# Six PSUM banks as one tile in an attention and SwiGLU layer, with priority for what empties a bank and later input builds

## The chip, the cores and the metric

The kernel runs on one core of one Trainium2 chip. The metric is the device time of one execution, in microseconds (us). A core has a matrix engine (TensorE, PE in the profile, with its weight loads as PEld), a vector engine (VectorE, DVE), a scalar engine (ScalarE, ACT), a general engine (GpSimd, POOL) and a queue engine (SyncE, SP) from which this kernel issues nearly all its transfers. TensorE writes its results to PSUM, which has eight banks of 128 partitions x 512 fp32 values; VectorE and ScalarE read them there.

## The reference

One layer of a streaming encoder on x, 2048 tokens of width 1024, in float32. The layer adds two normalised branches to x:

```python
h = rms_norm(x, g_pre_mix);  m = chunk_relpos_attention(h, w_qkv, w_o, rel_bias)
x = x + rms_norm(m, g_post_mix)
h = rms_norm(x, g_pre_ffn)
x = x + rms_norm((silu(h @ w_gate) * (h @ w_up)) @ w_down, g_post_ffn)     # 1024 -> 2816 -> 1024
```

The attention has 16 heads of width 64. Tokens stand in chunks of 64, and a query reads its own chunk and the eight before it, with a learned bias by clipped distance:

```python
for c in range(n_chunks):                       # 32 chunks of 64 queries
    k0, k1 = max(0, (c - 8) * 64), (c + 1) * 64
    sc = q[c] @ k[k0:k1].T / 8 + bias
    out[c] = softmax(sc) @ v[k0:k1]
```

## The kernel before, in words

**Tiles and stages.** The tokens are cut into four quarters of 512. Dense products run as three products of split numbers (a high and a low part for each operand, lines 197 to 199), and the large ones (values, queries and keys, gate and up, down) use a scheme of seven block products on 2 x 2 blocks, named B11, B21, T1, T2, B22, T3 and T4; the class `Blocks` builds their inputs with ACT and DVE. In time the kernel runs: projections for two groups of two quarters (`project`, 0 to 498.7 us), attention (498.7 to 1107), the output projection of the last quarter (`o_quarter`, from 1107), and the feed-forward part up to the end.

**Attention.** Quarters run in the order 1, 0, 2, 3. In each, eight jobs of one pair of heads run, and each job has four slots of 128 queries. A slot `t` of the loop issues:

- `transposed(t)`: four 128 x 128 transposes of the first head's probabilities, then four of the second's (L548). DVE copies the first to SBUF (L551), ACT the second (L553).
- `scaled(t + 2)`: DVE takes a reciprocal of the row sums (L530), POOL scales two heads' probabilities (L533).
- `scores(t + 3)`: eight matmuls (L508 and L509) write two heads' scores, 640 keys each. DVE adds the bias and reduces, one instruction per head (L517); ACT takes the exponential, one per head (L521).
- `fifth(t)`: the fifth key block's two transposes (L562), copied by ACT (L563). Quarter 0 has no earlier quarter, so its slots have fewer key blocks and no fifth.
- every fourth slot, `output()`: PV of the job before, 32 matmuls (L578) into `po`; ACT copies it as the high part (L584), and DVE subtracts that for the low part (L585).

Between these, `fill` puts in dense matmuls of the output projection of the quarter before, three at a time. The first quarter that runs has no such work.

**PSUM in attention.** Pool `psa` holds `st` (three banks, one buffer, the scores of both heads), `tt` (one bank, two buffers) and `po` (one bank). Two more banks belong to pool `ps` (tag "mm", two buffers), which the dense work uses.

**What sets the order.** PE runs in the order of the code (a manual schedule). The other engines' instructions are ordered by the tile framework's scheduler, by priority, which follows the order of the code unless a block of code raises it. Semaphores between the engines are put in by the framework, from the tiles that an instruction reads and writes. Work on other engines that prepares a later stage stands in a list `later`; `tick` takes it off as PE's work is issued, at a cost that each step names. Weights come by `fetch` (two 512 KB loads on SP's queue) and are split by `part_split` (L131 on ACT, L132 on DVE).

Of the kernel before, what the change touches and what calls it, by code (L numbers as in the profile page):

```python
# [17 lines left out]
P = 128  # L18
# [31 lines left out]
def trunk(  # L50
# [18 lines left out]
    class sp:  # L69
        @staticmethod  # L70
        def dma_start(dst, src):
            last_sp[0] = nc.sync.dma_start(dst, src)

# [370 lines left out]

    class Attend:


        def __init__(self, n, p):
            self.n, self.p = n, p
            self.prev = n > 0  # L450
            self.sc = {}
            self.pT = None

# [37 lines left out]
        def scores(self, ib):  # L491
# [19 lines left out]
            for h in range(2):  # L511
# [5 lines left out]
                dve.tensor_tensor_reduce(  # L517
# [19 lines left out]
        def transposed(self, ib):  # L537
# [6 lines left out]
            for h in range(2):  # L544
                part = blocks[:4]
                tt = phase["psa"].tile([P, 4, P], F32, tag="tt", name="tt", bufs=2)
# [3 lines left out]
                if h == 0:  # L550
                    dve.tensor_copy(dst, tt[:, : len(part), :])  # L551
                else:
                    act.activation(dst, tt[:, : len(part), :], AF.Copy)  # L553
            self.rest = (sc, blocks[4], cols) if self.prev else None

        def fifth(self):
# [6 lines left out]
            act.activation(self.pT[:, :, 4, cols], tt[:, 0:2, :], AF.Copy)  # L563

        def output(self):
# [8 lines left out]
            po = phase["psa"].tile([P, HALF], F32, tag="po", name="po", bufs=1)  # L574
# [9 lines left out]
            act.activation(ats[n].hi(p), po, AF.Copy)  # L584
            return lambda: dve.tensor_tensor(ats[n].lo(p), po, ats[n].hi(p).bitcast(F32), op=ALU.subtract)  # L585

    def o_quarter(n):
# [4 lines left out]
        for d2 in range(KT // 2):  # L592
# [3 lines left out]
            for dt in (2 * d2, 2 * d2 + 1):  # L596
# [10 lines left out]
                act.activation(t, pt, AF.Copy)  # L607
# [3 lines left out]
    class Blocks:  # L611
# [53 lines left out]
        def put(self, name, k, src):  # L665
            if name not in self.t:
                self.t[name] = hb_tile(self.slot[name])
            split(self.t[name][:, 0, k, :], self.t[name][:, 1, k, :], src)

        def build(self, part, w, prep):  # L670
# [17 lines left out]

            def b11(k):
                prep(0, k, at("T3", 1, k))  # L690
                self.put("B11", k, at("T3", 1, k))

            def b21(k):
                prep(0, k + 4, at("T4", 1, k))
                self.put("B21", k, at("T4", 1, k))

            def t1(k):
# [3 lines left out]
                self.put("T1", k, a)  # L701

            def t2(k):
# [3 lines left out]
                dve.tensor_tensor(a, c, a, op=ALU.add)  # L707
                self.put("T2", k, a)
                dve.tensor_tensor(b, b, c, op=ALU.subtract)
                dve.tensor_tensor(a, d, a, op=ALU.subtract)  # L710
# [205 lines left out]
    def gate_up(g, b):  # L916
# [22 lines left out]
        for c in range(NC):  # L939
# [6 lines left out]
            def copy(pts, dst):  # L946
                return lambda i: act.activation(dst[i], pts[i], AF.Copy)
# [4 lines left out]
            def c11(i):  # L952
                if i == 0:
                    t["B11"] = narrow("b11")
                    act.activation(t["B11"], pa[0], AF.Silu)
                else:
                    finish(t["B11"], pa[1])
                    put("B11")

            def u(i):  # L960
                dve.tensor_tensor(u2[i], p1[i], pb[i], op=ALU.subtract)
                dve.tensor_tensor(p5[i], p5[i], p1[i], op=ALU.add)

            def closing(pts, terms, then, op=ALU.subtract):
                def go(i):
                    dve.tensor_tensor(terms[i], pts[i], terms[i], op=op)  # L966
# [47 lines left out]
    def down(g, store, between=lambda n: None):  # L1014
# [42 lines left out]
        def copy(pts, to):  # L1057
            return lambda d, _: act.activation(to[d], pts[d], AF.Copy)

        def add(a, b_, op=ALU.add):  # L1060
            return lambda dst: dve.tensor_tensor(dst, a, b_, op=op)
# [17 lines left out]
        def u(d, _):  # L1079
            if not end:  # L1080
                u2[d] = narrow("u2")
            dve.tensor_tensor(u2[d], p1[d], pc[d], op=ALU.subtract)
# [10 lines left out]
        def c22(d, _):  # L1093
            dve.tensor_tensor(u3[d], pc[d], p1[d], op=ALU.subtract)
# [83 lines left out]
    def values_of(g, b, big):  # L1178
# [4 lines left out]
        def put(n, m, u, a, b_, op=ALU.add):  # L1183
            t = narrow("v")
            dve.tensor_tensor(t, a, b_, op=op)
            emit_v(n, m, u, t)

        def after(name, m, pt):
            if name == "B11":
                act.activation(p1[m], pt, AF.Copy)  # L1190
            elif name == "B21":
                put(s0, m, 0, pt, p1[m])
            elif name == "T1":
                act.activation(z[m], pt, AF.Copy)
# [482 lines left out]
```

## Time and profile before

| | |
|---|---|
| runs (us) | 2447.67, 2444.43, 2446.71; median 2446.71 |
| profiled execution (us) | 2446.41 |
| its span in the profile (us) | 2444.6 |
| mean granted clock of TensorE | 0.991 |
| PE busy | 2347.2 us, 96% of the span, 11480 matmuls |
| DVE, ACT, POOL busy | 1644.1, 1163.2 and 316.7 us |
| DMA | 529.72 MB, mean 217 GB/s |

A row of the windows view gives a stretch's length, then for PE, PEld, DVE, ACT and POOL the busy time and (x) the instructions, then the clock that TensorE was granted as a share of full speed, the share of the DMA engines that was busy, and GB/s. A row of the timeline gives start, length, engine, line and operation, output <- inputs, shape; in brackets stands the idle time before it and the instruction that ended it. A group's row gives line, engine, operation and count, then busy time and the mean of one in ns, then the idle time before. Ends of matmuls are modelled, and consecutive matmuls overlap, so the step from one start to the next is read for their cost in a row.

### The profile page before, as it was taken

The numbers are of one execution on the slowest core, as the hardware profiler recorded it, in microseconds if no ns is written. First come the engines' busy times: TensorE is split into PE (matmuls) and PEld (weight loads), VectorE is DVE, ScalarE is ACT, GpSimd is POOL, SyncE is SP. The second block draws the span as 40 slices with busy tenths as digits, with TensorE's granted clock in tenths as the row PEclk, the third lists the DMA queues.
The fourth block names the chain that finished last, engine by engine and source line by source line (L and its number), as shares of the span: only waits on it lengthen the run. The fifth ranks groups of instructions, "written<-read, shape, count | busy, mean of one in ns | idle before, by whom it ended". The sixth has DMA issues, their size and how long they took to land.

```text
span 2444.6 us, 33016 instructions
## 1 busy us (share of the span) xinstructions
PE 2347.2 (96%) x11480; PEld 1903.1 (78%) x11480; DVE 1644.1 (67%) x2625; ACT 1163.2 (48%) x2039; POOL 316.7 (13%) x422
## 2 busy tenths in 40 slices
PE   8999899989999899998999999999999999999998
PEld 6887688866676676767887888888888888888887
DVE  7775856666665556667876777677657667555567
ACT  8443733357665555664433333365433333334454
POOL 1012110023334324330000000000000000000002
PEclk9999999999999999999999999999999999999999
DMA  7699997678798878946666544287666757446654
GB/s 281 215 293 311 306 274 233 186 208 226 198 230 234 261 207 227 246 139 235 230 210 238 194 173 167 101 268 240 213 219 202 235 158 239 137 169 233 193 187 153
DMA packets 229782, 529.72 MB, mean 217 GB/s; under 512 B 26320, under 2 KB 42720, under 8 KB 225136
## 3 DMA queue, kind: packets, MB, share of 16 engines
q1 hardware_dynamic: 217712, 480.42, 62.6%
q0 software_dynamic: 11904, 47.19, 6.5%
q8 instruction: 91, 1.49, 0.3%
q14 instruction: 75, 0.61, 0.1%
HBM read 380.14 MB, written 170.44 MB: 225 GB/s over the span
## 4 chain that ended last, share of the span: by engine, by line
PE 54%; DVE 2%; issue 2%; DMA 1%; ACT 1%; POOL 0%; SPq 0%; DVEq 0%; ACTq 0%; POOLq 0%
PE pd L199 6%; PE pd L198 6%; PE pd L197 6%; PE pb L197 4%; PE pb L199 4%; PE pb L198 4%; PE pc L199 3%; PE pc L198 3%; PE pc L197 3%; PE pa L198 3%; PE pa L199 3%; PE pa L197 3%; PE po L578 1%; PE mm L199 1%; PE mm L197 1%
## 5 line engine op out<-in xcount | busy, mean ns | idle before, releaser
L533 POOL TENSOR_SCALAR sc<-sc,rows 128x640 f32<-128x640 f32 (+4 forms) x256 | 195.6, 777 | 364.7 <-DVE rows L530 221.9
L521 ACT ACTIVATE sc<-sc,rows 128x640 f32<-128x640 f32 (+4 forms) x256 | 192.9, 755 | 88.6 <-DVE rows L517 88.1
L517 DVE CUSTOM_DVE_ANT_0 sc<-st,bias 128x640 f32<-128x640 f32 (+2 forms) x248 | 173.6, 734 | 57.0 <-PE st L509 31.9
L197 PE MATMUL pb<-hb,w_wg_T 128*128 128x512 f32 x528 | 206.4, 391 | 3.8 <-DVE terms L966 3.8
L199 PE MATMUL pb<-hb,w_wg_T 128*128 128x512 f32 x528 | 206.2, 391 | 0.0
L198 PE MATMUL pb<-hb,w_wg_T 128*128 128x512 f32 x528 | 206.1, 390 | 0.0
L548 PE MATMUL tt<-ident,sc 128*128 128x128 f32 x928 | 135.0, 278 | 34.3 <-DVE pT L551 10.2
L548 PEld LDWEIGHTS tt<-ident,sc 128*128 128x128 f32 x928 | 105.1, 141 | 76.9 <-issue 45.0
L508 PE MATMUL st<-k,q 128*128 128x384 f32 (+3 forms) x432 | 137.4, 338 | 14.4 <-DVE rows L517 13.1
L199 PE MATMUL pd<-a,w_d_T 128*128 128x512 f32 (+1 forms) x368 | 139.9, 380 | 0.1
L197 PE MATMUL pd<-a,w_d_T 128*128 128x512 f32 (+1 forms) x368 | 139.9, 380 | 0.0
L198 PE MATMUL pd<-a,w_d_T 128*128 128x512 f32 (+1 forms) x368 | 139.8, 380 | 0.0
L551 DVE COPY pT<-tt 128x512 f32<-128x512 f32 (+3 forms) x128 | 81.5, 637 | 83.7 <-PE tt L548 63.6
L198 PE MATMUL pa<-hb,w_wg_B 128*128 128x512 f32 x352 | 136.9, 389 | 0.0
L197 PE MATMUL pa<-hb,w_wg_B 128*128 128x512 f32 x352 | 136.9, 389 | 0.0
L199 PE MATMUL pa<-hb,w_wg_B 128*128 128x512 f32 x352 | 136.9, 389 | 0.0
L968 ACT ACTIVATE terms<-terms 128x512 f32<-128x512 f32 x65 | 41.1, 632 | 182.5 <-DVE terms L966 182.5
L131 ACT ACTIVATE w_wg_T<-raw 128x1024 fp32r<-128x1024 f32 x88 | 92.9, 1057 | 71.9 <-PE pa L199 35.1
L509 PE MATMUL st<-k,q 128*128 128x384 f32 (+3 forms) x432 | 126.9, 314 | 0.0
L354 DVE TENSOR_TENSOR a<-raw_a,a 128x512 fp32r<-128x512 f32 x154 | 105.5, 692 | 25.2 <-ACT a L353 24.8
L289 POOL TENSOR_TENSOR rs<-ms,neg_half 128x4 f32<-128x4 f32 (+1 forms) x7 | 8.4, 1201 | 863.9 <-DVE ms L287 863.9
L197 PEld LDWEIGHTS pb<-hb,w_wg_T 128*128 128x128 f32 x528 | 99.5, 188 | 25.8 <-issue 4.6
(265 smaller groups left out, 6248.9 us busy)
## 6 DMA issues: line engine op xcount, KB each, us to landing
raw<-in_w_gu SPq DMA_DIRECT2D x77, 512.0 KB, 4.2
q<-q SPq DMA_DIRECT2D x62, 512.0 KB, 6.7
k<-k SPq DMA_DIRECT2D x54, 512.0 KB, 9.0
s_g_S<-raw POOLq DMA_DIRECT2D x44, 512.0 KB, 3.0
raw_d<-d_S SPq DMA_DIRECT2D x88, 256.0 KB, 3.6
raw_a<-aT SPq DMA_DIRECT2D x88, 256.0 KB, 3.5
raw<-s_g_S SPq DMA_DIRECT2D x44, 512.0 KB, 4.2
bias<-ext_d SPq DMA_DIRECT2D x124, 144.0 KB, 9.0
```

Source lines behind the costliest of these rows:

```text
L131: act.activation(hi, raw, AF.Copy)
L197: pe.matmul(pt, a_hi, b_hi, start=first, stop=False, skip_group_check=go_on)
L198: pe.matmul(pt, a_hi, b_lo, start=False, stop=False, skip_group_check=go_on)
L199: pe.matmul(pt, a_lo, b_hi, start=False, stop=last, skip_group_check=go_on)
L354: eng.tensor_tensor(lo, src, hi.bitcast(F32), op=ALU.subtract)
L508: pe.matmul(st[:, a:b], q[:, 2 * h, cols], kk[:, h, key], start=True, stop=False)
L509: pe.matmul(st[:, a:b], q[:, 2 * h + 1, cols], kk[:, h, key], start=False, stop=True)
L517: dve.tensor_tensor_reduce(out=sc[:, :n], in0=st[:, c0 : c0 + n], in1=rev, scale=-1.0, scalar=3.0e38, op0=ALU.add, op1=ALU.min, accum_out= ...
L521: act.activation(sc[:, :n], sc[:, :n], AF.Exp, bias=nmax, scale=-1.0, accum_out=rows[:, h : h + 1])
L533: last_pool[0] = pool.tensor_scalar(sc[:, :n], sc[:, :n], rows[:, 2 + h : 3 + h], 1.0, op0=ALU.mult, op1=ALU.mult)
L548: pe.transpose(tt[:, u, :], sc[h][:, b * P : b * P + P], ident)
L551: dve.tensor_copy(dst, tt[:, : len(part), :])
```

## The change

Five things change.

1. `Soon` wraps ACT and DVE so that an instruction issued through it has the scheduler's priority of 150 instructions earlier. It is used for what reads a PSUM bank: the reductions of scores, the copies of transposes and PV, and the first readers of the block products. In the changed kernel such instructions have the helper's line, L85.
2. One tile of six banks, `banks`, takes the place of `st`, `tt` and `po`. In the quarters after the first, the scores take banks 0 to 2, and the first head's transposes, the second's, the fifth block's and PV take banks 3, 4 and 5 in turn. In the first quarter the transposes of four go to the "mm" buffers of pool `ps`, the fifth block's to bank 4 and PV to bank 5, and each head's scores are cut as 512 + 128, in banks 0 and 1 for the first head and 2 and 3 for the second. Before, and in the later quarters, they are cut as 384 + 256 and 256 + 384, and the two heads share the middle bank.
3. In `project` the 32 ACT instructions that scaled x by the gain are gone; the gain is a factor of the instructions that build the blocks (an ACT copy with a scale, and a DVE scalar-tensor-tensor). The warm-up matmuls go from 28 to 20, and the steps for the row roots of group 0 and 1 wait longer between by-token sums and their transposes (2 to 14, and 2 to 8 units).
4. The second group's blocks are built later: B21 behind product B22 of the first group's queries and keys (it was T2), and T1, T2, B22, T4 and T3 behind T4, so in the second group's values (T1 and T2 were built behind B22 and T3).
5. Before the last quarter's output projection, its first weights are fetched behind the first of four row loads instead of behind all four.

```diff
+    class Soon:
+        def __getattr__(self, name):
+            op = getattr(self.eng, name)
+            def call(*args, **kw):
+                with tc.high_priority(offset=150):
+                    return op(*args, **kw)
+            return call
+    act_soon, dve_soon = Soon(act), Soon(dve)
...
+    def banks():
+        if "banks" not in phase:
+            phase["banks"] = phase["psa"].tile([P, 6 * HALF], F32, name="banks", bufs=1)
+        return phase["banks"]
...
+        def bank(self, name):
+            if self.alone and name != "t5":
+                return ps.tile([P, HALF], F32, tag="mm", name="tt")
+            if self.alone:
+                at = 4
+            else:
+                at = 3 + turn_of[0] % 3
+                turn_of[0] += 1
+            return banks()[:, at * HALF : at * HALF + HALF]
...
-            if "S" not in phase:
-                phase["S"] = phase["psa"].tile([P, 3 * HALF], F32, name="st", bufs=1)
-            st = phase["S"]
+            st = banks()
+            if self.alone:
+                cuts = [(0, 512, 640), (1024, 1536, 1664)]
...
-                dve.tensor_tensor_reduce(
+                dve_soon.tensor_tensor_reduce(
...
-                tt = phase["psa"].tile([P, 4, P], F32, tag="tt", name="tt", bufs=2)
+                tt = self.bank("tt").rearrange("p (a b) -> p a b", a=4)
...
-                    dve.tensor_copy(dst, tt[:, : len(part), :])
+                    dve_soon.tensor_copy(dst, tt[:, : len(part), :])
...
-            tt = phase["psa"].tile([P, 4, P], F32, tag="tt", name="tt", bufs=2)
+            tt = self.bank("t5").rearrange("p (a b) -> p a b", a=4)
...
-            po = phase["psa"].tile([P, HALF], F32, tag="po", name="po", bufs=1)
+            po = banks()[:, 5 * HALF : 6 * HALF] if self.alone else self.bank("po")
...
-            act.activation(ats[n].hi(p), po, AF.Copy)
-            return lambda: dve.tensor_tensor(ats[n].lo(p), po, ats[n].hi(p).bitcast(F32), op=ALU.subtract)
+            act_soon.activation(ats[n].hi(p), po, AF.Copy)
+            return lambda: dve_soon.tensor_tensor(ats[n].lo(p), po, ats[n].hi(p).bitcast(F32), op=ALU.subtract)
...
-        def put(self, name, k, src):
+        def put(self, name, k, src, scale=None):
...
+            act.activation(hi, src, AF.Copy, scale=scale)
+            dve.scalar_tensor_tensor(lo, src, scale, hi.bitcast(F32), op0=ALU.mult, op1=ALU.subtract)
...
             elif name == "T2":
-                dve.tensor_tensor(p1[m], p1[m], pt, op=ALU.subtract)
-                dve.tensor_tensor(z[m], z[m], p1[m], op=ALU.add)
+                dve_soon.tensor_tensor(p1[m], p1[m], pt, op=ALU.subtract)
+                dve_soon.tensor_tensor(z[m], z[m], p1[m], op=ALU.add)
...
-        for _ in range(28):
+        for _ in range(20):
...
-                act.activation(x_, x_, AF.Copy, scale=gt[:, PRE_MIX, k : k + 1])
...
-            (1.0, build(0, "B21", 2.5)), (14.0, build(0, "T1", 3.5)[:1]), (17.0, roots(0, 2.0)),
-            (20.0, build(0, "T1", 3.0)[1:]), (30.0, build(0, "T2", 3.5)), (45.0, roots_by_tokens(1, 0.5, 2.0, spare)),
+            (1.0, build(0, "B21", 2.5)), (14.0, build(0, "T1", 3.5)[:1]), (17.0, roots(0, 14.0)),
+            (20.0, build(0, "T1", 3.0)[1:]), (30.0, build(0, "T2", 3.5)), (45.0, roots_by_tokens(1, 0.5, 8.0, spare)),
...
-                elif name == "T2":
+                elif name == "B22":
                     later.extend(timed((0.5, build(1, "B21", 1.8))))
-                elif name == "B22":
-                    later.extend(timed((0.5, build(1, "T1", 1.8))))
-                elif name == "T3":
-                    later.extend(timed((0.5, build(1, "T2", 3.0))))
                 elif name == "T4":
                     later.extend(timed(
-                        (20.0, build(1, "B22", 3.0)), (34.0, build(1, "T4", 3.0)), (50.0, build(1, "T3", 2.0)),
+                        (1.0, build(1, "T1", 2.5)), (14.0, build(1, "T2", 4.0)), (31.0, build(1, "B22", 3.0)),
+                        (44.0, build(1, "T4", 3.0)), (57.0, build(1, "T3", 2.0)),
                     ))
...
         first(part, 0.0)[0][1]()
+        if part == "L11":
+            fetch()
```

On PE the order of the matmuls in attention stays, and what they wait for changes. The rows below are a slot of the third quarter with PV behind it, before: transposes, scores, a dense product (mm), and the fifth block's transposes. `Activation_49`, `DVE_49` and `Pool_49` are the semaphores of ACT, DVE and POOL.

```order
L548 MATMUL tt<-ident,sc 128x128 [waits Activation_49,Pool_49]
L548 MATMUL tt<-ident,sc 128x128 x3
L548 MATMUL tt<-ident,sc 128x128 [waits Activation_49,Pool_49]
L548 MATMUL tt<-ident,sc 128x128 x3
L508 MATMUL st<-k_4_7298,q_4_7297 128x384 [waits DVE_49]
...
L199 MATMUL mm<-hb_24_5647,w_1_7084 128x512
L562 MATMUL tt<-ident,sc 128x128 [waits DVE_49]
L562 MATMUL tt<-ident,sc 128x128
```

The same slot of the changed kernel:

```order
L584 MATMUL banks<-ident,sc 128x128 [waits Activation_49,Pool_49]
L584 MATMUL banks<-ident,sc 128x128 x3
L584 MATMUL banks<-ident,sc 128x128 [waits DVE_49,Pool_49]
L584 MATMUL banks<-ident,sc 128x128 x3
L544 MATMUL banks<-k_4_7120,q_4_7119 128x384 [waits Activation_49]
...
L216 MATMUL mm<-hb_24_5566,w_1_6918 128x512
L598 MATMUL banks<-ident,sc 128x128 [waits DVE_49]
L598 MATMUL banks<-ident,sc 128x128
```

The second head's transposes now wait for DVE, and the scores for ACT. The values that these semaphores are compared with belong to the copy of the first head's transposes (DVE) and the copy of the second head's (ACT), both of this slot; the first transposes' ACT value belongs to the fifth block's copy of the slot before, and the fifth block's DVE value to the second reduction of this slot's scores.

In the first quarter the rows of PE were, from the second head's transposes on:

```order
L548 MATMUL tt<-ident,sc 128x128 [waits Activation_49,Pool_49]
L548 MATMUL tt<-ident,sc 128x128 x3
L508 MATMUL st<-k_1_4130,q_1_4129 128x384 [waits DVE_49]
...
L562 MATMUL tt<-ident,sc 128x128 [waits DVE_49]
L562 MATMUL tt<-ident,sc 128x128
L578 MATMUL po<-pT,hb_20_3913 64x512 [waits DMAHW7_49]
```

and are now, with `tt` in pool `ps`:

```order
L584 MATMUL tt<-ident,sc 128x128 [waits Activation_49,Pool_49]
L584 MATMUL tt<-ident,sc 128x128 x3
L544 MATMUL banks<-k_1_4098,q_1_4097 128x512 [waits Activation_49]
...
L598 MATMUL banks<-ident,sc 128x128 [waits DVE_49]
L598 MATMUL banks<-ident,sc 128x128
L614 MATMUL banks<-pT,hb_20_3881 64x512 [waits DMAHW7_49,Activation_49]
```

The scores wait for ACT's copy of the fifth block of the slot before, in place of DVE's reduction, and PV waits for ACT's copy of the fifth block too.

On SP, ahead of the last quarter's output projection, the queue issued four row loads of 1 MB (x into hb) and then the weights (w_o into raw):

```order
L72 DMA hb_29_10150<-x_0_83 128x2048
L72 DMA hb_30_10152<-x_0_83 128x2048
L72 DMA hb_29_10150<-x_1_84 128x2048
L72 DMA hb_30_10152<-x_1_84 128x2048
L72 DMA raw_0_10157<-in_w_o 128x1024
L72 DMA raw_1_10159<-in_w_o 128x1024
```

and now issues:

```order
L72 DMA hb_29_9798<-x_0_83 128x2048
L72 DMA raw_0_9800<-in_w_o 128x1024
L72 DMA raw_1_9802<-in_w_o 128x1024
L72 DMA hb_30_9804<-x_0_83 128x2048
L72 DMA hb_29_9798<-x_1_84 128x2048
L72 DMA hb_30_9804<-x_1_84 128x2048
```

The first two weight loads stand ahead of three of the row loads.

More of the change, by code (lines that the diff above doesn't have):

```diff
@@ L72, in dma_start, with __init__ @@
             last_sp[0] = nc.sync.dma_start(dst, src)
+    class Soon:
+        def __init__(self, eng):
+            self.eng = eng
+        def __getattr__(self, name):
[5 more added lines that the diff above has]
+    act_soon, dve_soon = Soon(act), Soon(dve)
     const = ctx.enter_context(tc.tile_pool(name="const", bufs=1))
@@ L550, in transposed @@
                 if h == 0:
-                    dve.tensor_copy(dst, tt[:, : len(part), :])
+                    dve_soon.tensor_copy(dst, tt[:, : len(part), :])
                 else:
-                    act.activation(dst, tt[:, : len(part), :], AF.Copy)
+                    act_soon.activation(dst, tt[:, : len(part), :], AF.Copy)
             self.rest = (sc, blocks[4], cols) if self.prev else None
@@ L663, in norm, with build @@
             )
-        def put(self, name, k, src):
+        def put(self, name, k, src, scale=None):
             if name not in self.t:
                 self.t[name] = hb_tile(self.slot[name])
-            split(self.t[name][:, 0, k, :], self.t[name][:, 1, k, :], src)
-        def build(self, part, w, prep):
+            hi, lo = (self.t[name][:, n, k, :] for n in range(2))
+            if scale is None:
+                split(hi, lo, src)
+                return
+            act.activation(hi, src, AF.Copy, scale=scale)
+            dve.scalar_tensor_tensor(lo, src, scale, hi.bitcast(F32), op0=ALU.mult, op1=ALU.subtract)
+        def build(self, part, w, prep, lazy=False):
             def raw(name, half, t, k0, each=1):
@@ L687, in build, with gain, joined @@
                 return [(w, raw(*loads[part[:3]], 1 if part[3:] else 4))]
-            def b11(k):
-                prep(0, k, at("T3", 1, k))
-                self.put("B11", k, at("T3", 1, k))
-            def b21(k):
-                prep(0, k + 4, at("T4", 1, k))
-                self.put("B21", k, at("T4", 1, k))
+            def gain(k):
+                return gt[:, self.gain, k : k + 1] if lazy else None
+            def joined(out, one, k, other, op):
+                if lazy:
+                    dve.scalar_tensor_tensor(out, one, gain(k), other, op0=ALU.mult, op1=op)
+                else:
+                    dve.tensor_tensor(out, one, other, op=op)
+            def b11(k):
+                if not lazy:
+                    prep(0, k, at("T3", 1, k))
+                self.put("B11", k, at("T3", 1, k), gain(k))
+                if lazy:
+                    prep(0, k, at("T3", 1, k))
+            def b21(k):
+                if not lazy:
+                    prep(0, k + 4, at("T4", 1, k))
+                self.put("B21", k, at("T4", 1, k), gain(k + 4))
+                if lazy:
+                    prep(0, k + 4, at("T4", 1, k))
             def t1(k):
@@ L700, in t1 @@
                 dve.tensor_tensor(a, a, b, op=ALU.subtract)
-                self.put("T1", k, a)
+                self.put("T1", k, a, gain(k))
             def t2(k):
@@ L706, in t2 @@
                 prep(1, k + 4, c)
-                dve.tensor_tensor(a, c, a, op=ALU.add)
+                if lazy:
+                    act.activation(c, c, AF.Copy, scale=gain(k + 4))
+                joined(a, a, k, c, ALU.add)
                 self.put("T2", k, a)
-                dve.tensor_tensor(b, b, c, op=ALU.subtract)
-                dve.tensor_tensor(a, d, a, op=ALU.subtract)
+                joined(b, b, k, c, ALU.subtract)
+                joined(a, d, k + 4, a, ALU.subtract)
             def b22(k):
@@ L965, in go @@
                 def go(i):
-                    dve.tensor_tensor(terms[i], pts[i], terms[i], op=op)
+                    dve_soon.tensor_tensor(terms[i], pts[i], terms[i], op=op)
                     if i == 0:
@@ L1184, in put @@
             t = narrow("v")
-            dve.tensor_tensor(t, a, b_, op=op)
+            dve_soon.tensor_tensor(t, a, b_, op=op)
             emit_v(n, m, u, t)
@@ L1189, in after @@
             if name == "B11":
-                act.activation(p1[m], pt, AF.Copy)
+                act_soon.activation(p1[m], pt, AF.Copy)
             elif name == "B21":
@@ L1248, in go @@
                 def go(i):
-                    dve.tensor_tensor(terms[i], pts[i], terms[i], op=op)
+                    dve_soon.tensor_tensor(terms[i], pts[i], terms[i], op=op)
                     emit_qk(n, p, i, terms[i], terms[i])
@@ L1293, in prep @@
                     add_square(x_, totals[0], k == 0)
-                act.activation(x_, x_, AF.Copy, scale=gt[:, PRE_MIX, k : k + 1])
             return prep
         def build(g, part, w=0.0):
-            return groups[g].build(part, w, prepare(g))
+            return groups[g].build(part, w, prepare(g), True)
         def now(steps):
```

30 lines of the change are left out of this document (16 added, 14 removed).

## The prediction, made before the changed kernel ran

> **What bounds the kernel now.** I read the page's first part, then the busy time of each engine stage by stage, then TensorE's waits, then the timeline of single attention slots. The first rows are the page's line of engines and the windows of five stretches (length, then busy time and instructions of PE, PEld, DVE, ACT and POOL, the granted clock, the DMA share and GB/s).
>
> ```profile
> PE 2347.2 (96%) x11480; PEld 1903.1 (78%) x11480; DVE 1644.1 (67%) x2625; ACT 1163.2 (48%) x2039; POOL 316.7 (13%) x422
> ...
> 200.00:280.00 80.00, 69.96 (x295) 55.87 (x294) 61.21 (x89) 43.22 (x68) 14.33 (x19) 0.96 0.96 301
> 498.70:645.90 147.20, 128.04 (x856) 93.01 (x854) 91.24 (x229) 96.78 (x221) 53.11 (x70) 0.98 0.80 213
> 645.90:738.30 92.40, 92.30 (x544) 71.37 (x545) 60.15 (x187) 59.65 (x168) 30.85 (x56) 1.00 0.90 228
> 738.30:1107.00 368.70, 333.14 (x2140) 257.37 (x2139) 220.73 (x471) 219.35 (x477) 136.23 (x150) 0.99 0.79 221
> 1402.00:2430.00 1028.00, 1027.86 (x4582) 852.64 (x4581) 679.24 (x954) 423.16 (x649) 17.95 (x22) 1.00 0.59 194
> ```
>
> TensorE bounds it: it is idle for 2444.6 - 2347.2 = 97.4 us in all. The feed-forward part from 1402 on has nothing left to give, nor has the second attention quarter (0.1 us idle in 645.9 to 738.3). Idle time lies in the first quarter (19.2 us), the third and fourth (35.6 us) and at a few points of the dense stages. The waits view of PE says what ended it (total us, times, longest):
>
> ```profile
> PE st L508 <- DVE rows L517: 18.1, 31, 3.3
> PE tt L548 <- DVE pT L551: 10.2, 11, 1.4
> PE tt L548 <- DVE rows L530: 8.6, 7, 2.5
> PE tt L548 <- ACT pT L563: 7.7, 11, 1.1
> PE prs L349 <- POOL hr L289: 5.5, 1, 5.5
> PE pb L197 <- ACT hi L435: 4.5, 1, 4.5
> PE pb L197 <- DVE terms L1249: 3.8, 2, 2.2
> PE pb L197 <- DVE terms L966: 3.8, 2, 3.5
> PE mm L197 <- ACT w L131: 3.2, 1, 3.2
> PE mm L199 <- DVE w L132: 2.3, 1, 2.3
> ```
>
> **The change part by part: the shared tile.** Before, scores, transposes and PV have tiles of their own (st, two of tt, po), and PE's wait for scores is one for DVE's reduction of the last scores. Now all are slices of one six-bank tile. The order of the changed program shows what PE waits for, and it isn't the bank: the second head's transposes (another bank than the first head's) wait for DVE's copy of the first, the scores (banks 0 to 2) for ACT's copy of the second, the fifth block's two for DVE's second reduction of the scores just made, the next slot's first transposes for ACT's copy of the fifth block, PV for that copy too, and the transposes behind PV for ACT's copy of PV. Each time it is the newest reader of the tile. So a write to any bank stands behind the last read of every bank, and what ran side by side runs in one chain. I cost the chain with a slot of the third quarter as it runs now:
>
> ```profile
> 869.15 0.60 PE L548 MATMUL tt<-ident,sc 128*128 128x128 f32 x4
> 869.78 0.69 DVE L551 COPY pT<-tt 128x512 f32<-128x512 f32 x1 [0.37 <-PE tt L548]
> ...
> 870.62 0.63 PE L548 MATMUL tt<-ident,sc 128*128 128x128 f32 x4 [0.88 <-DVE pT L551]
> ...
> 871.01 0.42 PE L508 MATMUL st<-k,q 128*128 128x384 f32 x1
> ...
> 871.29 0.60 ACT L553 ACTIVATE pT<-tt 128x512 f32<-128x512 f32 x1 [0.58 <-PE tt L548]
> ...
> 872.27 0.39 PE L197 MATMUL mm<-hb,w 128*128 128x512 f32 x1
> ...
> 874.06 0.08 DVE L517 DVE_READ_ACCUMULATOR2_ANT rows<- 128x1 f32 x1
> ...
> 874.26 0.81 ACT L521 ACTIVATE sc<-sc,rows 128x640 f32<-128x640 f32 x1
> ...
> 875.07 0.36 ACT L563 ACTIVATE pT<-tt 128x256 f32<-128x256 f32 x1
> ```
>
> Here one such wait happens to be there already: from first transposes over DVE's copy to the next transposes is 870.62 - 869.15 = 1.47 us, with 0.15 from the copy's end (870.47) to PE's start. Without a wait four transposes take 871.01 - 870.62 = 0.39. The step from second transposes over ACT's copy to scores becomes 871.29 + 0.60 + 0.15 - 870.62 = 1.42 in place of 0.39. The scores take 872.27 - 871.01 = 1.26. Behind them DVE reduces until 874.14, ACT's exponentials (one per head) run until 875.07, ACT copies the fifth block until 875.43, and 0.15 later PE may go on: 3.31 after the scores. The dense matmuls (six of about 0.39) and the fifth block's transposes fit in that time. A slot is 1.47 + 1.42 + 1.26 + 3.31 = 7.46 us. Every fourth has PV:
>
> ```profile
> 860.96 4.53 PE L578 MATMUL po<-pT,v 128*64 128x512 f32 x32
> ...
> 865.53 0.60 ACT L584 ACTIVATE hb<-po 128x512 fp32r<-128x512 f32 x1 [2.41 <-PE po L578]
> ...
> L585 DVE TENSOR_TENSOR hb<-po,hb 128x512 fp32r<-128x512 f32 x17 | 11.6, 680 | 0.0
> ```
>
> That adds 4.53, ACT's copy (865.53 + 0.60 + 0.15 - 865.49 = 0.79), and some 0.2 of DVE's subtraction (0.68 long), which the fifth block's wait now includes: 5.5. A job of four slots becomes 4 x 7.46 + 5.5 = 35.3 us. Before, by the starts of PV:
>
> ```profile
> 541.26 0.65 PE L578 MATMUL po<-pT,hb 128*64 128x512 f32 x2
> ...
> 557.78 0.65 PE L578 MATMUL po<-pT,v 128*64 128x512 f32 x2
> ...
> 768.04 0.65 PE L578 MATMUL po<-pT,v 128*64 128x512 f32 x2
> ...
> 1083.40 0.65 PE L578 MATMUL po<-pT,v 128*64 128x512 f32 x2
> ```
>
> From 768.04 to 1083.40 are 14 jobs: 22.5 each. The growth is 12.8 x 14 = 179, with the first job (13) and the last (7) **+200** for the third and fourth quarter.
>
> **First quarter.** Its transposes go to tiles of their own (two "mm" banks), so only the chain scores, reductions, exponentials, fifth copy stays. The scores are cut 512 + 128 instead of 384 + 256, the same columns: 1.26, to 1.5 if a narrow matmul has a floor; I take 1.4. "Heads apart" gains nothing: PE reports once, behind the last of the eight matmuls, so DVE begins no earlier. Slot 1.4 + 3.31 = 4.71; with PV 4.71 + 4.53 + 0.79 = 10.03; about 0.4 more in the slot behind. A job is 3 x 4.71 + 10.03 + 0.4 = 24.5 against 557.78 - 541.26 = 16.5 now: 8.0 x 7, and 2 in the first, **+58**.
>
> **Second quarter.** There is no fifth block, so both transposes wait and the rest is covered by dense matmuls. The copies are shorter here (groups of 645.9 to 738.3):
>
> ```profile
> L551 DVE COPY pT<-tt 128x256 f32<-128x256 f32 (+3 forms) x28 | 13.6, 486 | 7.7 <-PE tt L548 7.7
> ...
> L553 ACT ACTIVATE pT<-tt 128x384 f32<-128x384 f32 (+3 forms) x27 | 11.6, 431 | 4.1 <-PE tt L548 4.0
> ```
>
> In the third quarter the wait cost 1.47 - 0.39 = 1.08 for a copy of 0.69, so copy + 0.39, and 1.42 - 0.39 = 1.03 for one of 0.60, so copy + 0.43. That is 0.88 + 0.86 = 1.74 per slot; 32 slots make 55.7. Eight jobs wait for PV's two readers, 0.79 and about 1.0: 14. PE had no slack to pay from: **+70**.
>
> Attention in all: **+328**. Bounds: the hand-overs of 0.15 are from few rows, and the engines' order within a slot can shift. 0.5 us per slot of the third and fourth quarter is 64 slots x 0.5 = 32; the same relative error in the rest is 13. So +283 to +373.
>
> [...] The trace of before shows separate tiles not waiting for each other (871.01: scores begin before ACT's copy of tt at 871.29) and has no row of two banks of one tile.
>
> **The other edits** gain. Priority lets what empties a bank go ahead of other work on ACT and DVE, which answers L1249 and L966 (3.8 each). Later builds of group two and the 32 scalings that ACT loses make room in 200 to 280 (L435, 4.5). Weights fetched ahead of three 1 MB loads on SP's queue answer the two waits on w (3.2 + 2.3); what is queued behind these two 512 KB loads are row loads that have until their block's preparation, and nobody waits for them in the view. Group one's root moves twelve units of work later on PE (prs, 5.5). That is 23.1 together. The clock comes with it: 0.04 x 80 = 3.2 in 200 to 280, and as much estimated for the start and the other two points: **-30**. Bounds: -45 when the small waits beside go too, and 0 when each wait is only replaced by the next transfer.
>
> **Sum.** 328 - 30 = +298 on the profiled execution of 2446.4 us, which lies 0.3 below the median: 2744; and some 6 for clock windows that fall (next part). I say **2750 us**.
>
> **Rivals.** The clock first:
>
> ```profile
> 211.25:214.66 3.41, 1.63 (x8) 1.01 (x6) 3.41 (x5) 1.69 (x2) 0.00 (x0) 1.00 0.80 223
> ...
> 501.44:504.86 3.42, 1.44 (x8) 1.12 (x8) 2.05 (x7) 1.73 (x4) 0.16 (x1) 0.99 0.66 153
> 504.86:508.27 3.41, 1.80 (x7) 1.80 (x8) 1.72 (x5) 1.73 (x4) 1.96 (x3) 0.50 0.91 229
> ```
>
> *The clock falls in attention (14%).* A window with PE busy 1.44 of 3.42 (0.42) is followed by one at half clock; one with 1.63 of 3.41 (0.48) is not. In the changed kernel PE is busy about 20.4 of 35.3 us (0.58), and a window over both transposes' waits and the scores comes to about 0.45. If one window in three of the 700 us fell, some 230 us at half clock with PE's work of 0.58 doubled would add up to 133, of which the chain hides a third: +95, **2845 us**. [...] The third quarter's gaps of today (35.6 us idle at a mean clock of 0.99) speak against it.
>
> *The fifth block's chain is hidden (13%).* If ACT copied the fifth block ahead of the second exponential, the way behind the scores shrinks from 3.31 to about 2.5, covered by PE's own 2.5 of work; slots become 6.7, the first quarter's near 3.9. That takes 0.8 x 96 slots = 77 and more where PV overlaps: **2640 us**. The built order has ACT's copy behind both exponentials in most slots, which is against it.
>
> *The waits don't bind, the other side (5%).* If the hardware's events let the banks work apart, or the named readers have always finished in time, the three rotating banks remove the waits on tt (10.2 + 8.6 + 7.7, say 25 of them with the clock), wider scores cost 4, and the gains of 30 stay: 2446 - 51 = **2395 us**. It decides as soon as tt's second transposes start within 0.4 of the first. Against it: 870.62 shows PE waiting for just such a copy where the program names it.
>
> *The change of attention as forecast, but no gain elsewhere* is within the range: 2780.
>
> **How the numbers follow.** Forecast 67%; clock 14, hidden fifth block 13, free banks 5, and 1 for no change. The likeliest's own range is 2690 to 2810 (attention's bounds with the gains' -30, and half of the gains' bounds). To take in the lighter cases of the clock and most of the hidden fifth block I give 2640 to 2840. Faster by over 0.2% (which is about what a measurement of this kernel tells from no change): 5%; within it 1%; slower 94%.
>
> **What would show it.** In the waits of PE, rows of scores, transposes and fifth block ended by the copies of DVE and ACT (now the helper's line) should hold some 300 us, and no longer a reduction of the slot before. PV starts should be 35 us apart in the third and fourth quarter and 24.5 in the first; a window of 645.9 to 738.3's kind should show PE idle for 70. The waits on prs, L435, and w should be gone. I am wrong if second transposes follow the first at 0.4 us, if PV's period in the third quarter is under 30, or if a stage's clock is under 0.9.

## The result

| | before | changed |
|---|---|---|
| median (us) | 2445.83 | 2861.93 |
| runs | 2444.43 to 2447.67 | 2861.30 to 2863.48 |
| span of the profiled execution (us) | 2444.6 | 2859.5 |
| mean granted clock | 0.991 | 0.938 |
| forecast | | 2750 (2640 to 2840) |

The ratio is 1.1702, with a 95% interval of 1.1681 to 1.1722: 416 us slower. The direction was forecast; the time lies 22 us above the range.

The page's line of engines, and the windows of the first, second, third with fourth quarter and of the rest (from the first scores, and from one PV to another):

```profile
PE 2518.9 (88%) x11464; PEld 1979.5 (69%) x11464; DVE 1650.9 (58%) x2625; ACT 1158.7 (41%) x2015; POOL 318.4 (11%) x422
...
488.50:731.60 243.10, 173.17 (x813) 127.34 (x813) 89.90 (x220) 95.63 (x216) 52.15 (x68) 0.72 0.48 128
731.60:926.90 195.30, 141.08 (x636) 95.31 (x636) 73.19 (x214) 73.21 (x190) 39.55 (x64) 0.88 0.53 141
926.90:1522.60 595.70, 410.25 (x2040) 276.67 (x2040) 212.89 (x447) 213.36 (x456) 127.18 (x143) 0.88 0.42 122
1522.60:2859.50 1336.90, 1319.72 (x5896) 1090.86 (x5896) 919.47 (x1271) 542.98 (x819) 43.02 (x57) 1.00 0.60 201
```

By the same marks (first scores; eighth, 16th and last start of PV) the kernel before took 498.7, 139.8, 109.1, 351.7 and 1345.3 us. So the changed kernel gained 10 us ahead of attention and 8 behind it, and lost 103, 86 and 244 us in attention's three parts. Two things show in these rows. PE is idle for 310 us of attention (70 + 54 + 185). And PE is *busy* there 178 us longer than before (724.5 against 546.5) with the same work, at a clock of 0.72 to 0.88: the matmuls themselves were slower (a first-quarter slot's eight for the scores took 2.82 us from 580.22, at a clock of 0.50, and 1.57 from 593.51, at 1.00).

The waits of PE name the pairs that the forecast named, now on the helper's line:

```profile
PE banks L598 <- DVE rows L85: 83.2, 68, 1.9
PE banks L544 <- ACT pT L85: 59.4, 93, 1.2
PE banks L584 <- DVE pT L85: 49.6, 59, 1.4
PE banks L598 <- DVE hb L85: 37.2, 23, 2.6
PE banks L584 <- POOL sc L569: 27.5, 29, 1.4
PE banks L584 <- ACT hb L85: 19.3, 24, 1.0
```

L598 is the fifth block, which waits for the reduction of scores just made (`rows`) or PV's low part (`hb`); L544 the scores, which wait for ACT's copy of transposes; L584 the transposes. With one exception, none of these is the reader of the bank that PE wants to write. The exception is `hb` in the third and fourth quarter (16 of the 23 times, 20.1 of the 37.2 us): there the turn over three banks gives the fifth block behind PV the bank that PV has just used, so PE would have to wait for its low part with separate banks too (in e6 below, with the same turn, the view has no such wait). The row that names POOL most likely stands for DVE's copy as well: where the view names DVE, the second head's transposes begin some 0.15 us behind the end of the copy (1167.43 and 1167.58), where it names POOL they do so too (1175.01 and 1175.15), and POOL is then scaling the probabilities of a later slot. Three neighbouring windows of the first quarter show the other half:

```profile
562.99:566.40 3.41, 1.32 (x8) 0.99 (x7) 3.10 (x7) 1.86 (x4) 0.00 (x0) 1.00 0.11 38
566.40:569.82 3.42, 2.87 (x12) 2.77 (x13) 1.36 (x3) 1.73 (x6) 1.58 (x2) 0.50 1.04 241
569.82:573.23 3.41, 1.55 (x11) 1.28 (x11) 1.58 (x4) 1.36 (x4) 0.00 (x0) 1.00 1.03 299
```

A window with PE busy 1.32 of 3.41 us is followed by one at half clock; there such work fills 2.87 us, the clock comes back, PE is done early and waits (1.55), and the next window falls again. The whole quarter goes on like this: 40 of its 71 windows are at half clock, one to five of them in a row.

### The profile page after: what moved, and what is told of

Same layout as the page of the kernel before. It is cut to its first block, busy times and chain, and to the rows that moved or that the text cites. A ratio compares the mean times of both kernels' runs of the same rounds, so it can differ in the third digit from the quotient of the medians.

```text
span 2859.5 us, 33183 instructions
## 1 busy us (share of the span) xinstructions
PE 2518.9 (88%) x11464; PEld 1979.5 (69%) x11464; DVE 1650.9 (58%) x2625; ACT 1158.7 (41%) x2015; POOL 318.4 (11%) x422
## 4 chain that ended last, share of the span: by engine, by line
PE 54%; DVE 7%; ACT 5%; issue 3%; DMA 2%; POOL 2%; SPq 0%; DVEq 0%; POOLq 0%; ACTq 0%
PE pd L216 5%; PE pd L215 5%; PE pd L214 5%; PE pb L214 4%; PE pb L216 4%; PE pb L215 4%; PE banks L614 3%; PE banks L584 3%; PE banks L544 3%; ACT sc L557 2%; PE pa L216 2%; PE pa L215 2%; PE pa L214 2%; PE pc L216 2%; PE pc L215 2%
## 5 line engine op out<-in xcount | busy, mean ns | idle before, releaser
L85 DVE CUSTOM_DVE_ANT_0 sc<-banks,bias 128x640 f32<-128x640 f32 (+2 forms) x248 | 173.3, 736 | 318.6 <-PE banks L545 291.5
L544 PE MATMUL banks<-k,q 128*128 128x384 f32 (+3 forms) x432 | 173.0, 411 | 59.4 <-ACT pT L85 59.4
L584 PE MATMUL banks<-ident,sc 128*128 128x128 f32 x672 | 116.7, 293 | 114.9 <-DVE pT L85 49.6
L584 PEld LDWEIGHTS banks<-ident,sc 128*128 128x128 f32 x672 | 77.9, 148 | 173.7 <-issue 106.6
L85 ACT ACTIVATE pT<-banks 128x512 f32<-128x512 f32 (+2 forms) x192 | 87.5, 456 | 193.1 <-PE banks L584 186.6
L544 PEld LDWEIGHTS banks<-k,q 128*128 128x128 f32 x432 | 102.8, 238 | 88.5 <-ACT pT L85 83.8
L545 PE MATMUL banks<-k,q 128*128 128x384 f32 (+3 forms) x432 | 156.3, 385 | 0.0
L598 PE MATMUL banks<-ident,sc 128*128 128x128 f32 x192 | 49.2, 345 | 121.1 <-DVE rows L85 83.2
L85 DVE COPY pT<-banks 128x512 f32<-128x512 f32 (+2 forms) x96 | 59.9, 624 | 151.1 <-PE banks L584 132.5
L614 PE MATMUL banks<-pT,v 128*64 128x512 f32 (+3 forms) x832 | 133.5, 477 | 9.3 <-ACT pT L85 6.5
L215 PE MATMUL pd<-a,w_d_T 128*128 128x512 f32 (+1 forms) x368 | 139.8, 380 | 0.0
L598 PEld LDWEIGHTS banks<-ident,sc 128*128 128x128 f32 x192 | 22.1, 161 | 159.7 <-DVE rows L85 110.0
```

The costliest lines, as they stand in the source:

```text
L85: return op(*args, **kw)
L215: pe.matmul(pt, a_hi, b_lo, start=False, stop=False, skip_group_check=go_on)
L544: pe.matmul(st[:, a:b], q[:, 2 * h, cols], kk[:, h, key], start=True, stop=False)
L545: pe.matmul(st[:, a:b], q[:, 2 * h + 1, cols], kk[:, h, key], start=False, stop=True)
L584: pe.transpose(tt[:, u, :], sc[h][:, b * P : b * P + P], ident)
L614: pe.matmul(po[heads[h], c0:c1], v[:, kb, c : c + 64], self.pT[:, h, r, c0:c1], start=m == 0, stop=m == len(terms) - 1,)
```

## The experiments

The theory after the result: (a) the one tile puts each write behind the newest read of any bank, and costs what the chain says at full clock; (b) the idle time that this makes brings the clock down in about a third of attention, for another 90 to 100 us; (c) the other edits gain. The rivals: the priority or the rotation over three banks makes the loss, or the half clock costs nothing, since DVE and ACT set the pace.

### Own tiles, the one tile alone, and neither

The changed kernel with tiles of their own:

```diff
-            phase["banks"] = phase["psa"].tile([P, 6 * HALF], F32, name="banks", bufs=1)
+            phase["banks"] = phase["psa"].tile([P, 3 * HALF], F32, name="st", bufs=1)
...
-            return banks()[:, at * HALF : at * HALF + HALF]
+            return phase["psa"].tile([P, HALF], F32, tag="tt", name=name, bufs=3)
```

> The changed kernel with all its other edits, but scores in a three-bank tile of their own and transposes, fifth block and PV in three one-bank tiles in turn (first quarter: the four transposes in the mm banks as in the change, scores cut as before the change). If the one tile makes the loss, attention (first to last PV: 998 us in the changed kernel, 575 before) comes back to 550 to 575 us and the time is 2405 to 2432 us: the 15 us that the changed kernel gained outside attention, and 0 to 25 of PE's waits in attention. If the rotation over three banks or the priority makes a part of the loss, it stays over 2500 us.

Measured: 2406.02 us, ratio 0.9852 (0.9831 to 0.9872). First to last PV took 554 us. The three banks in turn and the priority are still there, and nothing of the loss is.

The kernel before with the one tile alone:

```diff
-                phase["S"] = phase["psa"].tile([P, 3 * HALF], F32, name="st", bufs=1)
+            phase["banks"] = phase["psa"].tile([P, 6 * HALF], F32, name="banks", bufs=1)
...
-                tt = phase["psa"].tile([P, 4, P], F32, tag="tt", name="tt", bufs=2)
+                tt = self.bank("tt").rearrange("p (a b) -> p a b", a=4)
```

> The kernel before with the one six-bank tile alone: no priority, no edits in the projections, no earlier fetch. If the one tile makes the whole loss, PV's period is 37 to 38 us in the third and fourth quarter and 30 to 31 in the first, and the time is 2446 + 430 = 2865 to 2885 us. If the priority makes a part of it (reordering ACT and DVE in a slot), it is under 2830 us.

Measured: 2884.82 us, ratio 1.1807 (1.1783 to 1.1832), 443 us above the kernel before in these runs. PV's period is 30.4 to 31.0 us in the first quarter, and 36 to 40 in most jobs of the third and fourth. The one tile makes the whole loss; the priority has no part in it.

The changed kernel with the tiles and cuts of before:

```diff
+            tag, n = ("po", 1) if name == "po" else ("tt", 2)
+            return phase["psa"].tile([P, HALF], F32, tag=tag, name=tag, bufs=n)
```

> The changed kernel with the tiles of the kernel before (st, two tt, po, and the cuts of before): priority, projections and fetch are kept. If these edits gain what the changed kernel's stages outside attention show (6.6 us ahead of the first scores, 8.3 behind the last PV), the time is 2425 to 2435 us. By my forecast's term of -30 it would be 2416. If the priority hurts in attention, it is over 2446.

Measured: 2408.15 us, ratio 0.9859 (0.9837 to 0.9881): 34 us faster than the kernel before in the same runs. My expectation, made from the stages outside attention, missed by 17 us, since it left out what the other edits do in attention once the chain is gone: the third and fourth quarter took 335.4 us there against 351.7. Runs e7 and e8 below share these 16 us out: 9 with the priority alone, 6 without it. The term of -30 in the prediction was nearer. The rows of the waits that priority answered in the kernel before (transposes that wait for copies, 10.2 and 7.7 us, and behind a reciprocal, 8.6) have shrunk to one group of short ones:

```profile
PE st L533 <- DVE rows L85: 16.8, 24, 3.3
PE tt L573 <- ACT pT L85: 7.9, 26, 0.6
PE pb L214 <- DVE terms L85: 6.9, 3, 4.0
```

### Keeping TensorE busy

The chain and the clock act together, so one of them has to be held. These kernels keep the one tile's waits, and fill PE's idle time ahead of the waits with transposes of the identity into a spare bank that nobody reads. For the spare bank the one tile has five banks.

```diff
+    def busy(n):
+        banks()
+        for _ in range(n):
+            pe.transpose(phase["spare"][:, 0:P], ident, ident)
...
+            if not self.alone:
+                busy(6)
...
+                if h and not self.alone:
+                    busy(6)
...
+            busy(12 if self.alone else 8)
```

The three places are ahead of the scores, of the second head's transposes and of the fifth block.

> The changed kernel, with the one tile cut to five banks (two in turn behind the three for scores, and the first quarter's scores cut as before the change) and 128x128 transposes of the identity into a spare bank that nobody reads, issued ahead of PE's waits: 12 (about 1.2 us) ahead of the fifth block in the first quarter; later 8 ahead of the fifth block and 6 each ahead of the second transposes and the scores. The waits stay. If a half clock in a third of attention's time costs about 100 of the 416 us, the clock goes to 0.97 or more and the time to 2760 to 2800 us in spite of the added work. If the chain of DVE and ACT hides the slow matmuls, the time stays at 2850 to 2880 us, whatever the clock does.

Measured: 2768.05 us, ratio 1.1335 (1.1308 to 1.1362), clock 0.992. With two banks in turn, the transposes behind PV write over PV before its low part is read, so this kernel's output is not the layer's. The next run gives PV a bank of its own:

> Run e4_kept_busy again, with PV in a bank that no transposes take (there the second transposes of the next slot wrote over PV before its low part was read, so the output was not the reference's). The waits and instructions are the same: 2760 to 2775 us, half clock about 45 us as there. Anything over 2790 would mean that the time of e4 hung on the wrong data.

Measured: 2765.72 us, ratio 1.1303 (1.1275 to 1.1330), clock 0.993.

> As e4_kept_busy with half the filler (6 transposes ahead of the fifth block in the first quarter; later 4, 3 and 3), and PV in a bank that no transposes take, so PV's low part is read as in the changed kernel. In the changed kernel 65 windows of 3.41 us were followed by half clock, nearly all with PE busy 0.37 to 0.53 of the window; windows over 0.58 stayed. If that share decides, half the filler (0.6 us of a slot of 6 us in the first quarter, 1.0 of 7.5 later, so 0.10 to 0.14 more) lifts most windows over it: half clock under 100 us in all and 2765 to 2800 us. If it takes the full filler's share, half clock stays over 200 us and the time over 2820.

Measured: 2765.78 us, ratio 1.1306 (1.1269 to 1.1343), clock 0.992. So work that nobody needs, added to the changed kernel, makes it 96 us *faster*. Half of it does as much as the whole. In e4, e4c and e9 the first quarter's scores are also cut as before, which is worth little: at full clock their eight matmuls take 1.44 us in e9 and 1.57 in the changed kernel, so about 4 us in 32 slots (the prediction supposed steps of 1.26 and 1.4). The windows of the three parts of attention with half the filler:

```profile
486.90:686.70 199.80, 147.80 (x1014) 113.85 (x1012) 90.64 (x222) 95.71 (x216) 52.86 (x68) 0.96 0.58 157
686.70:865.60 178.90, 143.81 (x828) 102.37 (x828) 73.17 (x214) 73.18 (x190) 39.55 (x64) 1.00 0.56 154
865.60:1428.80 563.20, 427.87 (x2671) 310.45 (x2672) 212.77 (x447) 213.21 (x456) 126.88 (x143) 0.99 0.44 129
```

The clock is 0.96, 1.00 and 0.99 in place of 0.72, 0.88 and 0.88. In the changed kernel the three parts spent about (2 x 0.28 x 243) + (2 x 0.12 x 195) + (2 x 0.12 x 596) = 326 us at half clock, a third of attention. With the clock up, the chain can be read as it was worked out. A slot of the third quarter with half the filler:

```profile
1093.73 0.63 PE L591 MATMUL banks<-ident,sc 128*128 128x128 f32 x4
...
1094.46 0.69 DVE L85 COPY pT<-banks 128x512 f32<-128x512 f32 x1 [1.18 <-PE banks L591]
1095.30 0.63 PE L591 MATMUL banks<-ident,sc 128*128 128x128 f32 x4 [0.62 <-DVE pT L85]
...
1095.96 0.60 ACT L85 ACTIVATE pT<-banks 128x512 f32<-128x512 f32 x1 [2.38 <-PE banks L591]
1096.62 0.45 PE L549 MATMUL banks<-k,q 128*128 128x384 f32 x1 [0.36 <-ACT pT L85]
...
1097.90 0.40 PE L214 MATMUL mm<-hb,w 128*128 128x512 f32 x1
...
1100.80 0.36 ACT L85 ACTIVATE pT<-banks 128x256 f32<-128x256 f32 x1
...
1101.31 0.63 PE L591 MATMUL banks<-ident,sc 128*128 128x128 f32 x4 [0.24 <-ACT pT L85]
```

First to second transposes 1.57 us (forecast 1.47), to the scores 1.32 (1.42), the scores 1.28 (1.26), to the next slot 3.41 (3.31): 7.58 in place of 7.46.

### Which links of the tile cost what

The scores get their own tile again; transposes, fifth block and PV keep one of three banks.

```diff
-            phase["banks"] = phase["psa"].tile([P, 6 * HALF], F32, name="banks", bufs=1)
+            phase["banks"] = phase["psa"].tile([P, 3 * HALF], F32, name="banks", bufs=1)
+            phase["S"] = phase["psa"].tile([P, 3 * HALF], F32, name="st", bufs=1)
```

> The changed kernel with the scores in a three-bank tile of their own (cut as before the change); transposes, fifth block and PV share one three-bank tile. The links from a copy to the scores and from the reduction to the fifth block are gone; those between the transposes, the fifth block and PV stay. By my chain a slot of the third quarter is 1.47 + 0.39 + 1.26, then exponentials, fifth copy and restart 3.3: 6.4 in place of 7.5 us, the first quarter is as before, the second pays 0.88 a slot: 2540 to 2600 us. If the links to the scores are the whole loss: under 2450. If the links among the transposes are the whole: over 2700.

Measured: 2547.94 us, ratio 1.0426 (1.0406 to 1.0447), clock 0.991. Against e1 (2406) the links among transposes, fifth block and PV cost 142 us. The links to the scores, which the changed kernel has on top, cost the remaining 314, most of the clock's 96 among them, since e6 kept a clock of 0.991. PV's period in the third and fourth quarter is mostly 27 us; I had 4 x 6.4 + 5.5 = 31, so the time lies in the range though the slot was wrong. The 6.4 had ACT's copy of the fifth block behind both exponentials. In e6 the fifth block no longer waits for a reduction, and ACT copies it ahead of the second exponential in 61 of the 64 slots (in the changed kernel in 4). The links that I took for gone are (the waits of PE hold no row of the fifth block on `rows`), and those that stay are in front:

```profile
PE banks L584 <- DVE pT L85: 52.3, 58, 2.4
PE banks L584 <- DVE rows L566: 28.2, 29, 1.5
PE banks L584 <- ACT hb L85: 19.0, 23, 1.2
PE banks L584 <- ACT pT L85: 16.9, 26, 0.7
PE st L544 <- DVE rows L85: 15.5, 18, 2.2
```

### Heads apart with waits that follow

In the changed kernel "heads apart" could not work: both heads' banks belong to one tile, and DVE's first reduction began behind the last of the eight matmuls (at 595.26, where that one ran from 594.81 to 595.08). Here each head has its own.

```diff
-            st = banks()
+                st = phase["psa"].tile([P, 2 * HALF], F32, tag="st", name=f"st{h}", bufs=2)
...
-            return phase["psa"].tile([P, HALF], F32, tag="tt", name=name, bufs=3)
+            return phase["psa"].tile([P, HALF], F32, tag="tt", name=name, bufs=2)
```

> The kernel of run e1_own_tiles with heads apart in a way that the program's waits follow: each head's scores have a two-bank tile of their own (two buffers), and transposes, fifth block and PV share two one-bank tiles in place of three. If PE reports a head's scores when they are done and DVE may begin 0.6 us earlier, the waits of the scores on DVE (22 us, 24 times in e1) mostly go: first quarter's job 15 us or less against 16.5, time 2388 to 2400 us. If two buffers are too few for the four users, the third and fourth quarter (165 us each in e1) grow and the time is 2410 us or more.

Measured: 2413.13 us, ratio 0.9877 (0.9861 to 0.9894). DVE does begin early: at 561.92, when the first head's scores are done and the second's are being made.

```profile
561.79 0.34 PE L533 MATMUL st<-k,q 128*128 128x384 f32 x1
...
561.92 0.82 DVE L85 CUSTOM_DVE_ANT_0 sc<-st,bias 128x640 f32<-128x640 f32 x1 [0.77 <-PE st L533]
561.97 0.28 PE L532 MATMUL st<-k,q 128*128 128x256 f32 x1
```

But the first quarter did not get shorter (142.3 us from the first scores to the eighth PV, against 141.3 in e1). In its stretch of the trace PE's waits moved from the reductions (16.3 us, 18 times, in e1) to POOL, which scales the probabilities:

```profile
PE tt L572 <- POOL sc L557: 16.0, 8, 2.0
PE st L532 <- DVE rows L85: 3.7, 2, 2.6
```

So neither branch of the expectation holds as I put it. The gain is missing in the first quarter, where PE waits for POOL in the place of DVE; the third and fourth quarter did not grow (331.5 us against 330.3), and the second did by 3.

### The other edits apart

> The kernel before with the priority alone (tiles, projections and fetch as before). Run e3 was 14 us shorter ahead of attention, 16 in the third and fourth quarter, 11 behind the last PV. If priority makes the part in attention (copies of transposes go ahead of other work on ACT and DVE) and half of the last: 2418 to 2428 us. If the earlier fetch and the projections make nearly all (my forecast gave priority two waits, 7.6 us): 2433 to 2441.

Measured: 2435.52 us, ratio 0.9966 (0.9952 to 0.9979), so 7 to 8 us. The third and fourth quarter took 342.7 us in place of 351.7. Ahead of attention it lost 4: the transposes of the row roots wait longer for POOL, 8.8 us where it was 5.5.

```profile
PE prs L366 <- POOL hr L306: 8.8, 1, 8.8
PE pb L214 <- DVE terms L85: 3.6, 1, 3.6
```

The edit for e8 is the other way round:

```diff
             def call(*args, **kw):
-                with tc.high_priority(offset=150):
-                    return op(*args, **kw)
+                return op(*args, **kw)
```

> Run e3 without the priority: projections and fetch changed, tiles as before. By my forecast's shares (L435, prs, the clock in 200 to 280, the waits on w) it is 2415 to 2425 us. If priority is worth about 20 us, it is 2425 to 2432.

Measured: 2428.07 us, ratio 0.9930 (0.9906 to 0.9954), 14 us faster than before; its four executions spread from 2419 to 2430. Together with e7 that is 21 us, and e3, which has both, gained 34. A part of the difference has a place: alone, priority makes the wait on the row roots longer, and with the projections' edits that wait is gone. In the third and fourth quarter priority alone also brings new waits, for a sum on DVE (6.4 us) and for loads of keys (6.0), which come to 7.6 in e3. Whether this is all was not tried.

### Three banks in turn everywhere

```diff
-            if self.alone and name == "tt":
-                return ps.tile([P, HALF], F32, tag="mm", name="tt")
```

> Run e1_own_tiles, with the first quarter's transposes in the same three one-bank tiles as the rest, not in the mm banks. The first quarter took 141.3 us in e1 and 139.2 in e3 (two tt tiles and po): 2403 to 2407 us if that difference goes, 2408 or more if three tiles are too few for the first quarter.

Measured: 2406.56 us, ratio 0.9833 (0.9806 to 0.9859). The first quarter stays at 141.3 us, so the time fell into the first branch of the expectation without its reason. So e1, e3 and e10 can't be told apart: rotation over three one-bank tiles, with PV in the turn, is worth nothing measurable over two tiles and one for PV. All three are 1.4 to 1.7% faster than the kernel before and 16% faster than the changed one.

## Why the prediction was right and wrong

**The mechanism held.** The waits are those named, the one tile alone makes the loss (e2), own tiles undo it (e1), and with the clock held each term of the chain's sum is close:

| term | forecast | measured near full clock (e9 against before) |
|---|---|---|
| slot of the third quarter | 7.46 us | 7.58 |
| PV's period, first quarter | 24.5 | 24.0 in three, 24.6 to 25.7 in three |
| PV's period, third and fourth | 35.3 | 35.3 to 36.7 |
| first quarter | +58 | 199.8 - 139.8 = +60 |
| second quarter | +70 | 178.9 - 109.1 = +70 |
| third and fourth | +200 | 563.2 - 351.7 = +212 |

The sum is +342 against the forecast's +328, inside its bounds of 283 to 373. These are figures of a kernel with filler, and in the first quarter with the cuts of before; what the chain alone costs the changed kernel at full clock was not measured.

**The other edits** gain 34 us without the tile (e3), and the term said 30, so its size was right, but not its shares. The two waits on `terms` (3.8 each) that priority was to end are still there (8.2 us in four waits in the changed kernel), and the 16 us that come in the third and fourth quarter had no term. In the changed kernel itself only the 10 us ahead of attention and the 8 behind it show; the 16 can't show where the one tile's chain sets the pace.

**The step that failed** is the clock: "I say 2750", with "some 6 for clock windows that fall", and the fall itself as a rival at 14%. Measured it is 96 us (2861.9 against 2765.8 with half the filler), net of the filler and some 4 of them the cuts', and 326 us at half clock where the rival supposed 230. That the rival's price was 95 is partly luck: its time at half clock was too short, and its 133 less a third is 89. It also worked with a job of the third quarter, while the clock fell deepest in the first: 136 of the 326 us. The rival's time of 2845 was 17 short of the result, less than the chain's own miss and the gains that stayed away. What I had in hand was enough to see it: I put the fall between 0.42 and 0.48 of a window, worked out 0.45 for the chain's worst window, and then gave it a small chance because the third quarter of before kept its clock. But those gaps come now and then, and the chain's come in every slot. In the changed kernel windows of 0.39 and 0.45 come up again and again, since slots repeat.

**The hidden fifth block** (2640) and **free banks** (2395) did not happen in the changed kernel; the first came about in e6, where the links to the scores are gone. What the latter says of a kernel whose banks stand apart was right to 11 us (e1: 2406), reached with own tiles.

**What would show it**, as the prediction put it: behind the first quarter, second transposes never came 0.4 us after the first (0.77 at the least); PV's period was over 30; the six rows of waits above sum to 276 us, where I had some 300. A stage's clock under 0.9 was named there as the sign that the forecast is wrong, and that is what came.

## What to carry to other kernels

PSUM banks that are to be written and read side by side belong in tiles of their own: the framework's waits here followed the tile, and six banks in one tile turned four engines' overlapping work into a chain, for some +342 us near full clock. After a change in tiles, read in the built order which instruction each wait stands for before costing anything. And where a chain leaves the matrix engine busy for less than about half of a window in slot after slot, as here (0.39 and 0.45 again and again, a clock of 0.72 to 0.88, 96 us), the clock's fall is no rival but a term of the sum, to be worked out with every slot's share of a window.

## What was not expected of the hardware

**The clock fell on a share of a window, and not on a long gap.** The longest idle gap of PE in the changed kernel's attention is 2.65 us (566.96, behind DVE's `hb`). In its trace 65 windows of 3.41 us at full clock were followed by half clock. PE was busy for 0.15 to 0.46 of the window in 39 of them, 0.47 to 0.55 in 25, and 0.64 in one. The lowest share of a window that kept its clock was 0.47 (in e9 one kept it at 0.44). So the edge lay near a half here, with a band of some 0.08 in which both happened: with shares of 0.47 to 0.55 the clock fell behind 25 windows and stayed behind 17. The way back took more: of 103 windows at half clock, the 64 that were followed by full clock had PE busy for 0.83 of the window or more, and among the 39 that were not the share went up to 0.91.

**Transposes held the clock.** The filler of e9 is nothing but fp32 transposes, and with it the clock of the first quarter went from 0.72 to 0.96.

**Useless work paid.** Some 0.6 to 1.0 us of transposes a slot, put where PE would wait anyhow, took 96 us off. That is a measure, not an advice: with the tiles apart little such idle time is left (in e1 the waits of scores and transposes come to 29 us: 22.3, 5.2 and 1.5), and the kernel is 360 us faster still.
